# Scale on TensorE in four groups, shift on VectorE, and late constants moved into the first stage of a mixer and mixture-of-experts kernel

## The chip, the cores and the metric

The kernel runs on one core of a Trainium2 chip. The metric is the device time of one execution in microseconds (us). Five engines work in parallel, each through its own queue of instructions in order: PE (TensorE, matmuls; its weight loads are listed apart as PEld), DVE (VectorE), ACT (ScalarE), POOL (GpSimd) and SP (SyncE, which in this kernel only issues DMA loads). They wait for each other through semaphores. SBUF is the on-chip memory, PSUM holds what PE writes.

## The reference, cut to what matters

One layer: 256 tokens, width 1024, a modulated mixer and then 32 experts of which each token takes 4. The part that the change touches is the first line of the layer.

```python
cond = jax.nn.silu(c)
mod = cond @ w_ada[layer] + b_ada[layer]
sh_m, sc_m, g_m, sh_f, sc_f, g_f = [m[:, None, :] for m in jnp.split(mod, 6, axis=-1)]
h = rms_norm(x, norm_mix[layer]) * (1.0 + sc_m) + sh_m
x = x + g_m * hybrid_mixer(h, w_in[layer], ...)      # lru, diff attention, sliding-window attention
h = rms_norm(x, norm_ffn[layer]) * (1.0 + sc_f) + sh_f
x = x + g_f * moe_ffn(h, w_router[layer], b_router[layer], w1[layer], b1[layer], w2[layer], b2[layer])
```

So the mixer's input needs two vectors of 1024, the scale `sc_m` and the shift `sh_m`, each a product of the row `cond` with a 1024 x 1024 matrix, before the first projection can start.

## The kernel before

The mixer takes the first quarter of the time, the experts' weight stream the rest. In the mixer every weight block of 128 x 1024 is split into a high and a low part (`split`, whi by a cast on ACT L117, wlo by a subtraction on DVE L109), and each product is three matmuls (`mm3`, L124 to L126: high x high, low, low).

The first stage is the loop over d = 0..7 in `branches`; d is the chunk of 128 of the 1024 input channels. One pass of it (a "turn" here) is:

- Loads on SP: two halves of the modulation matrix for chunk d (`wada<-wad`, L198, 0.5 MB each) and the projection weights `wqkv[d]` (`wt<-wqkv`, L84, 0.9 MB). The `wt` blocks live in three slots, so a load waits until the turn three before has finished splitting its block. SP waits in its queue for that, and everything queued behind it waits too.
- `ada_rows`: 8 fp32 matmuls (L240; 16 records in the trace) that make scale and shift of the chunk as rows in four column groups, a copy on ACT (`rd`, L243), 2 matmuls with `pick` (L245) that turn the rows into columns, and DVE's `mod` (L247).
- `h_chunk`: A (L253), hd = x * A + shift (L255) on DVE, the high part of h by a cast on ACT (L256), the low part on DVE (L257).
- 24 matmuls (L124 to L126) in the order of the columns of `wqkv`: 12 against its first 1024 columns, 12 against the last 768. They add to seven banks of PSUM that stay open over all eight turns.

Ahead of turn 0 stand the root-mean-square of x (`normed_T`: a Square on ACT for each half of x, sqrt, reciprocal) and 16 transposes of the normed x (L229). After the loop come `csb` (`row_tile`, L526: silu(c) spread over all partitions by 8 matmuls, for the later modulation on DVE), `proj_ch(0)`, the norms of q and k, `late_constants` (rows, gw, wr, b1t, tri and the bias table `relb`), `attn_prepare` (the vector lambda), `bias_tiles` (a product with the bias table, an addition L265, a write to DRAM `scr` from POOL's queue and three loads `tz` of 0.5 MB each through POOL's queue), the projection for the window attention, the diff attention, the lru and the gates. The remaining modulation vectors are made on DVE by a fused product and sum over 1024 columns (L206, output `wada`, one per 128 channels; their loads are `wada<-wada`). `wch` are the 1 MB weight blocks of the later projections.

Nothing in the code fixes the order of instructions of one engine: the Tile framework's scheduler works it out from the program's order, priorities and its own estimate of when operands are ready, when the kernel is built. `tc.high_priority()` lifts what is written inside it. At run time each engine goes through its list strictly in that order.

Of the kernel before, what the change touches and what calls it, by code (L numbers as in the profile page):

```python
# [44 lines left out]
class Kernel:  # L45
# [82 lines left out]
    def constants(self):  # L128
        nc, a, const = self.nc, self.a, self.const
        self.x = self.keep.tile([128, 2, D], F32, name="x")  # L130
        for t in range(2):
            nc.sync.dma_start(out=self.x[:, t], in_=a["x"][t * 128:(t + 1) * 128])
# [42 lines left out]
    def silu_c(self):  # L175

        nc = self.nc
        c = self.col(C_C, 8)
        sc = self.mix.tile([128, 8], F32, name="sc")
        nc.scalar.activation(sc, c, AF.Tanh, scale=0.5)  # L180
        nc.vector.scalar_tensor_tensor(sc, sc, 1.0, c, op0=ALU.add, op1=ALU.mult)
        self.sc = sc
        self.pick = self.early.tile([128, 1], F32, name="pick")
        nc.vector.memset(self.pick, 0.0)
        for j in range(4):
            nc.vector.memset(self.pick[32 * j:32 * j + 1], 1.0)
        self.bm = self.early.tile([128, 8, 2], F32, name="bm")
        b = self.col(C_BADA, 16).rearrange("p (d s) -> p d s", s=2)
        nc.vector.tensor_scalar(self.bm[:, :, 0], b[:, :, 0], 1.0, None, op0=ALU.add)
        nc.vector.tensor_copy(self.bm[:, :, 1], b[:, :, 1])  # L190
        self.mod = self.keep.tile([128, 48], F32, name="mod")

    def ada_load(self, i, first=False):
        ws = []
        for j in range(2):
            ws.append(self.p4("wada") if first else self.p4p.tile([128, D], F32, name="wada", tag="wada", bufs=2))
            src = self.a["wad0"][i] if first else self.a["wada"][i - 8]
            self.nc.sync.dma_start(out=ws[j], in_=src[:, j * D:(j + 1) * D])  # L198
        return ws

    def ada(self, i, ws=None):

        nc = self.nc
        for j, w in enumerate(ws or self.ada_load(i)):
# [4 lines left out]
    def normed_T(self, out):  # L209
# [4 lines left out]
        for t in range(2):  # L214
            nc.scalar.activation(xn[t], self.x[:, t], AF.Square, accum_out=ss[:, t:t + 1])
        self.silu_c()
        rs = mw.tile([128, 2], F32, name="rs")
        self.rstd(rs, ss, D, mw, 2)
        for t in range(2):
            if t:  # L220
                nc.scalar.mul(xn[t], self.x[:, t], rs[:, t:t + 1])
            else:
                nc.vector.tensor_scalar(xn[t], self.x[:, t], rs[:, t:t + 1], None, op0=ALU.mult)
        for d2 in range(4):
            p = self.ps()
            for i in range(2):
                for t in range(2):
# [5 lines left out]
    def ada_rows(self, d, ws):  # L233
# [3 lines left out]
        p = self.ps()  # L237
        for k in range(8):
            j = k % 4
            nc.tensor.matmul(p[32 * j:32 * j + 32, :256], self.sc[:, k:k + 1].to_broadcast([128, 32]),  # L240
                             ws[k // 4][:, j * 256:(j + 1) * 256], start=(k < 4), stop=(k >= 4))
        r = self.mw.tile([128, 256], F32, name="rd")
        nc.scalar.copy(r, p[:, :256])  # L243
        for i in range(2):
            nc.tensor.matmul(p[:, 256 + i:257 + i], r[:, i * 128:(i + 1) * 128], self.pick, start=True, stop=True)  # L245
        m = self.mod[:, 2 * d:2 * d + 2]
        nc.vector.scalar_tensor_tensor(m, p[:, 256:258], 0.5, self.bm[:, d], op0=ALU.mult, op1=ALU.add)  # L247

    def h_chunk(self, x, d):
# [3 lines left out]
        nc.vector.tensor_mul(A, self.mod[:, 2 * d:2 * d + 1], self.col(C_NM + d))  # L253
# [307 lines left out]
    def branches(self, br, gl):  # L561
# [25 lines left out]
        self.csb = self.row_tile("silu", self.sc, self.mix)  # L587
# [13 lines left out]
        self.late_constants()  # L601
        self.attn_prepare()
        self.bias_tiles()
# [547 lines left out]
def layout(inp):  # L1151
# [20 lines left out]
    a["wad0"] = wa[:, 1::-1].reshape(8, 128, 2, 8, 128).transpose(3, 1, 0, 2, 4).reshape(8, 128, 2048)  # L1172
# [51 lines left out]
```

## Time and profile before

| | |
|---|---|
| three runs, median (lowest to highest) | 1238.14 us (1238.09 to 1239.74) |
| the profiled execution's own time | 1238.5 us |
| its span | 1236.7 us |
| busy in the span: PE, DVE, ACT | 1125.8 us, 452.7 us, 259.3 us |
| mean DMA rate over the span | 381 GB/s |
| loop over d, from its first matmul to its last | 17.7 to 74.1 us |
| first matmuls of the experts | about 302 us |

Times within the profile are counted from the start of the span. A busy PE is not a PE at its peak, and PE has two clock levels: 1.00 in the profile's clock column is 2.4 GHz, 0.50 is 1.2 GHz. The profile puts each wait down to the instruction that released it. Whole-kernel shares are of little use here, since the mixer is bound by PE and by the chains between engines, and the experts by DMA; the stages have to be read apart.

### The profile page before, as it was taken

How to read it: one execution, taken by the hardware profiler on the slowest of the kernel's cores; microseconds unless marked ns; L12 is line 12 of the kernel's file. 1: busy time of each engine (PE TensorE's matmuls, PEld its weight loads, DVE VectorE, ACT ScalarE, POOL GpSimd, SP SyncE). 2: the span in 40 equal slices, each digit the busy share in tenths (PEclk: the TensorE clock that was granted, in tenths of full speed). 3: DMA queues.
4: the chain of work that ended last, by engine and by line, in shares of the span. 5: the costliest groups of instructions: out<-in, count | busy, mean ns of one | idle time of the engine just before them, and what ended most of it. 6: DMA issues, size and time to landing. Idle time of an engine off the chain costs nothing.

```text
span 1236.7 us, 13932 instructions
## 1 busy us (share of the span) xinstructions
PE 1125.8 (91%) x5719; PEld 552.4 (45%) x5720; DVE 452.7 (37%) x892; ACT 259.3 (21%) x446; POOL 11.0 (1%) x19
## 2 busy tenths in 40 slices
PE   5998999998988999998989798979898989798987
PEld 4787989995333334332323242324233323332333
DVE  3477888974123231231213132403131222121232
ACT  4475668444101011100000010101010100100000
POOL 0000000000010000000000000000000000000000
PEclk9998999998999999999999999999999999999999
DMA  9688467885999999999999999999999999999996
GB/s 376 210 288 299 147 218 264 343 325 219 414 417 425 424 424 426 427 426 425 423 429 424 429 424 424 429 424 424 423 427 427 424 426 424 427 426 426 423 403 237
DMA packets 54718, 470.70 MB, mean 381 GB/s; under 512 B 6048, under 2 KB 8152, under 8 KB 21112
## 3 DMA queue, kind: packets, MB, share of 16 engines
q1 hardware_dynamic: 53112, 466.93, 91.9%
q0 software_dynamic: 528, 1.72, 0.4%
q10 hardware_dynamic: 1008, 1.09, 0.3%
q8 instruction: 47, 0.77, 0.3%
q14 instruction: 23, 0.19, 0.0%
HBM read 468.65 MB, written 1.07 MB: 380 GB/s over the span
## 4 chain that ended last, share of the span: by engine, by line
PE 55%; DMA 41%; DVE 2%; ACT 1%; issue 1%; SPq 0%; DVEq 0%; ACTq 0%
DMA wt<-w2h 31%; PE po L923 10%; PE mm L923 9%; PE ps L943 7%; DMA wt<-w1h 7%; PE ps L956 3%; PE mm L124 3%; PE mm L125 3%; PE mm L126 3%; PE ps L883 3%; DMA wada<-wada 2%; PE ps L850 1%; PE po L125 1%; PE po L126 1%; PE po L124 1%; PE ps L420 1%
## 5 line engine op out<-in xcount | busy, mean ns | idle before, releaser
L923 PE MATMUL po<-wt,xT 128*64 128x512 f32 x992 | 335.7, 599 | 29.1 <-DMA wt<-w1h 29.1
L923 PE MATMUL mm<-wt,xT 128*64 128x512 f32 x992 | 331.4, 594 | 0.0
L943 PE MATMUL ps<-wt,act 128*64 128x512 f32 x992 | 234.3, 614 | 43.0 <-DMA wt<-w2h 36.1
L949 DVE TENSOR_TENSOR y<-ps,gf 64x512 f32<-64x512 f32 x62 | 42.7, 689 | 352.2 <-PE ps L943 351.5
L923 PEld LDWEIGHTS po<-wt,xT 128*64 128x64 f32 x992 | 87.8, 136 | 169.3 <-issue 112.7
L943 PEld LDWEIGHTS ps<-wt,act 128*64 128x64 f32 x992 | 72.7, 140 | 190.0 <-issue 133.6
L923 PEld LDWEIGHTS mm<-wt,xT 128*64 128x64 f32 x992 | 93.0, 137 | 132.5 <-issue 130.8
L853 DVE TENSOR_TENSOR g<-ps,b1t 128x512 f32<-128x512 f32 x31 | 21.4, 691 | 242.9 <-PE ps L850 242.9
L109 DVE TENSOR_TENSOR wlo<-wt,whi 128x1024 fp32r<-128x1024 f32 x72 | 85.6, 1192 | 35.6 <-ACT whi L117 34.4
L117 ACT CAST whi<-wt 128x1024 fp32r<-128x1024 f32 x72 | 73.5, 1023 | 74.4 <-PE ps L126 27.7
L927 ACT COPY hg<-po 128x512 f32<-128x512 f32 x31 | 18.1, 585 | 302.3 <-PE po L923 256.2
L126 PE MATMUL mm<-h,wlo 128*128 128x256 f32 x256 | 73.7, 288 | 0.0
L125 PE MATMUL mm<-h,whi 128*128 128x256 f32 x256 | 73.5, 287 | 0.0
L124 PE MATMUL mm<-h,whi 128*128 128x256 f32 x256 | 73.4, 287 | 0.0
L856 ACT ACTIVATE ps<-g 128x512 f32<-128x512 f32 x31 | 18.6, 601 | 219.9 <-DVE g L854 219.9
L956 PE MATMUL ps<-y,swT 128*128 128x512 f32 (+1 forms) x128 | 58.2, 606 | 6.4 <-DVE y L949 6.4
L958 DVE TENSOR_TENSOR x<-x,ps 128x512 f32<-128x512 f32 x64 | 43.8, 687 | 18.9 <-PE ps L956 18.9
L124 PEld LDWEIGHTS mm<-h,whi 128*128 128x128 f32 x256 | 49.1, 192 | 1.4 <-issue 1.3
L125 PEld LDWEIGHTS mm<-h,whi 128*128 128x128 f32 x256 | 49.0, 191 | 1.1 <-issue 1.0
L126 PEld LDWEIGHTS mm<-h,wlo 128*128 128x128 f32 x256 | 49.0, 192 | 1.0 <-issue 1.0
L886 ACT ACTIVATE xT<-ps,B,A 128x256 f32<-128x256 f32 x32 | 17.3, 564 | 139.1 <-PE ps L883 138.7
L206 DVE CUSTOM_DVE_ANT_0 wada<-wada,silu,cols 128x1024 f32<-128x1024 f32 x32 | 40.8, 1275 | 7.8 <-DMA wada<-wada 7.8
(335 smaller groups left out, 1103.7 us busy)
## 6 DMA issues: line engine op xcount, KB each, us to landing
wt<-w1h SPq DMA_DIRECT2D x93, 2048.0 KB, 29.5
wt<-w2h SPq DMA_DIRECT2D x47, 2048.0 KB, 29.5
wt<-w1h SPq DMA_DIRECT2D x70, 1024.0 KB, 29.6
wt<-w2h SPq DMA_DIRECT2D x33, 1024.0 KB, 31.3
wt<-wch SPq DMA_DIRECT2D x16, 1024.0 KB, 6.7
wada<-wada SPq DMA_DIRECT2D x32, 512.0 KB, 4.7
wada<-wad SPq DMA_DIRECT2D x16, 512.0 KB, 9.4
wt<-wqkv SPq DMA_DIRECT2D x8, 896.0 KB, 8.7
```

The lines of the kernel that those rows point to most:

```text
L109: eng.tensor_tensor(lo, x, hi.bitcast(F32), op=ALU.subtract)
L117: self.nc.scalar.copy(hi, w)
L124: nc.tensor.matmul(out, lhs[0], rhs[0], start=start, stop=False)
L125: nc.tensor.matmul(out, lhs[0], rhs[1], start=False, stop=False)
L126: nc.tensor.matmul(out, lhs[1], rhs[0], start=False, stop=stop)
L206: nc.vector.tensor_tensor_reduce(out=w, in0=w, in1=self.csb, scale=0.5, scalar=self.col(C_BADA + c), op0=ALU.mult, op1=ALU.add, accum_out= ...
L883: nc.tensor.matmul(p[:, i * 256:(i + 1) * 256], self.xs[j][:, t, d * 128:(d + 1) * 128], sel[:, t], start=(t + j == 0), stop=(t + j == 2))
L923: nc.tensor.matmul(p[64 * hf:64 * hf + 64], xT[:, k, i * CAP:(i + 1) * CAP], w[:, (2 * j + hf) * 512:(2 * j + hf + 1) * 512], start=(k == ...
L943: nc.tensor.matmul(py[rows[hf]], act[:, (k % 4) * 2 + k // 4, :], w[:, (2 * i + hf) * 512:(2 * i + hf + 1) * 512], start=(k == 0), stop=(k ...
L949: nc.vector.tensor_mul(self.y[r, hf], py[r], self.gf[r, hf * 512:(hf + 1) * 512])
L956: nc.tensor.matmul(p, swT[r, i, t * 128:(t + 1) * 128], self.y[r, hf], start=True, stop=True)
L958: nc.vector.tensor_add(self.x[:, t, s], self.x[:, t, s], p)
```

## The change

- `constants`: the loads of x get high priority. `normed_T` is split into `normed` and `transposed_x`. The square of x's second half moves from ACT to DVE (a fused product and sum), the table for sqrt is loaded ahead by a dummy activation, and each half of x is normed by DVE and ACT together, 512 columns each.
- The modulation of chunk d is split by kind. `scales`: 8 matmuls of 128 columns a chunk (256 before) on TensorE, for a group of chunks at once: chunk 0 before turn 0, 1 and 2 before turn 1, 3 and 4 before turn 3, 5 to 7 before turn 5; then one copy, one `pick` matmul a chunk and A for the whole group. `shift`: one fused product and sum on DVE a chunk. Their weights are the new arrays `wsc` and `wsh` (0.5 MB a chunk each).
- `csb`, which the shift needs, is made at the start and not after the loop.
- `late_constants` and `attn_prepare` are called in turn 4 and `bias_tiles` in turn 5; before, all three came after the loop.
- The first `wqkv` block is loaded in two pieces.

The diff, cut to its core (in `layout`, `wad0` is replaced by `wsc` and `wsh`, which hold the same numbers):

```diff
+        with self.tc.high_priority():
+            for t in range(2):
+                nc.sync.dma_start(out=self.x[:, t], in_=a["x"][t * 128:(t + 1) * 128])
...
+    def p4_load(self, name, src):
+        w = self.p4("w" + name)
+        self.nc.sync.dma_start(out=w, in_=src)
+        return w
+
+    def shift(self, d, w):
+
+        c = 2 * d + 1
+        self.nc.vector.tensor_tensor_reduce(out=w, in0=w, in1=self.csb, scale=0.5, scalar=self.col(C_BADA + c),
+                                            op0=ALU.mult, op1=ALU.add, accum_out=self.mod[:, c:c + 1])
...
+        nc.scalar.activation(xn[0], self.x[:, 0], AF.Square, accum_out=ss[:, 0:1])
+        nc.vector.tensor_tensor_reduce(out=xn[1], in0=self.x[:, 1], in1=self.x[:, 1], scale=1.0, scalar=0.0,
+                                       op0=ALU.mult, op1=ALU.add, accum_out=ss[:, 1:2])
+        warm = mw.tile([128, 1], F32, name="warm")
+        nc.scalar.activation(warm, ss[:, 0:1], AF.Sqrt, bias=self.eps, scale=1.0 / D)
...
+            nc.vector.tensor_scalar(xn[t][:, :512], x[:, :512], r, None, op0=ALU.mult)
+            nc.scalar.mul(xn[t][:, 512:], x[:, 512:], r)
...
+    def scales(self, ds, ws):
+
+
+        nc = self.nc
+        p, n = self.ps(), len(ds)
+        for i, w in enumerate(ws):
+            for k in range(8):
+                j = k % 4
+                nc.tensor.matmul(p[32 * j:32 * j + 32, i * 128:(i + 1) * 128],
+                                 self.sc[:, k:k + 1].to_broadcast([128, 32]), w[:, k * 128:(k + 1) * 128],
+                                 start=(k < 4), stop=(k >= 4))
+        r = self.mw.tile([128, 384], F32, name="rd", bufs=1)[:, :n * 128]
+        nc.scalar.copy(r, p[:, :n * 128])
+        for i in range(n):
+            nc.tensor.matmul(p[:, 384 + i:385 + i], r[:, i * 128:(i + 1) * 128], self.pick, start=True, stop=True)
+        nc.vector.scalar_tensor_tensor(self.A1[:, ds[0]:ds[0] + n], p[:, 384:384 + n], 0.5,
+                                       self.bm[:, ds[0]:ds[0] + n], op0=ALU.mult, op1=ALU.add)
+        nc.vector.tensor_mul(self.A1[:, ds[0]:ds[0] + n], self.A1[:, ds[0]:ds[0] + n],
+                             self.col(C_NM + ds[0], n))
...
+        with self.tc.high_priority():
+            first = [self.p4_load("sc", a["wsc"][0])], self.p4_load("sh", a["wsh"][0])
+        self.silu_c()
+        self.csb = self.row_tile("silu", self.sc, self.mix)
+        xn, groups = self.normed(), {0: [0], 1: [1, 2], 3: [3, 4], 5: [5, 6, 7]}
         for d in range(8):
-            w = self.ada_load(d, first=True)
+            g = groups.get(d, [])
+            wg, wsh = first if d == 0 else ([self.p4_load("sc", a["wsc"][e]) for e in g],
+                                            self.p4_load("sh", a["wsh"][d]))
+            wt = self.take()[:, :1792]
+            for c in (slice(0, 1024), slice(1024, 1792)) if d == 0 else (slice(0, 1792),):
+                nc.sync.dma_start(out=wt[:, c], in_=a["wqkv"][d][:, c])
+            if g:
+                self.scales(g, wg)
+            self.shift(d, wsh)
             if d == 0:
-                self.normed_T(gl[:2])
-            wt = self.load(a["wqkv"][d])
-            self.ada_rows(d, w)
+                self.transposed_x(xn, gl[:2])
             self.h_chunk(gl[d // 4][:, d % 4], d)
+            if d == 4:
+                self.late_constants()
+                self.attn_prepare()
+            if d == 5:
+                self.bias_tiles()
...
-        self.csb = self.row_tile("silu", self.sc, self.mix)
...
-        self.late_constants()
-        self.attn_prepare()
-        self.bias_tiles()
```

The change moves instructions. First place: PE between turn 0 and turn 1. In the kernel before, PE makes the modulation of chunk 1, and already that of chunk 2, between the last matmuls of turn 0 (into `ps`, 256 columns) and the first of turn 1 (into `mm`):

```order
L125 MATMUL ps<-wlo,h_75 128x256
L126 MATMUL ps<-whi,h_76 128x256
L240 MATMUL ps<-wada,sc 32x256 x8
L245 MATMUL ps<-pick,rd 128x1 x2
L240 MATMUL ps<-wada,sc 32x256 x8
L124 MATMUL mm<-whi,h_75 128x512
L125 MATMUL mm<-wlo,h_75 128x512
```

In the changed kernel the scales of chunks 1 and 2 stand there together, and nothing follows their `pick` until turn 1:

```order
L125 MATMUL ps<-wlo,h_75 128x256
L126 MATMUL ps<-whi,h_76 128x256
L256 MATMUL ps<-wsc,sc 32x128 x16
L262 MATMUL ps<-pick,rd 128x1 x2
L124 MATMUL mm<-whi,h_75 128x512
L125 MATMUL mm<-wlo,h_75 128x512
```

The second set of L240, which made the modulation of a chunk one turn ahead, is gone; each group is made right before the turn that needs it.

Second place: SP's queue from turn 5's loads on. Before, modulation weights and projection weights of a chunk alternate to the last chunk, and only then the `wch` blocks come, with most late constants behind them:

```order
L198 DMA wada<-wad 128x1024 x2
L84 DMA wt<-wqkv 128x1792
L198 DMA wada<-wad 128x1024 x2
L84 DMA wt<-wqkv 128x1792
L84 DMA wt<-wch 128x2048 x2
L149 DMA rows<-rows 128x40
L152 DMA gw<-gw 128x1024
```

In the changed kernel the late constants stand ahead of the scales of chunks 5 to 7, and the last two shift loads (chunks 6 and 7) behind two `wch` loads:

```order
L161 DMA tri<-tri 128x128
L422 DMA lamv<-rows 128x256
L202 DMA wsc<-wsc 128x1024 x3
L202 DMA wsh<-wsh 128x1024
L597 DMA wt<-wqkv 128x1792 x3
L84 DMA wt<-wch 128x2048
L350 DMA lam<-cols 128x4
L197 DMA wada<-wada 128x1024
L84 DMA wt<-wch 128x2048
L202 DMA wsh<-wsh 128x1024 x2
L197 DMA wada<-wada 128x1024 x4
```

What moved: the weights that turns 6 and 7 need for their h stood ahead of all `wch` loads, and half of them now stand behind two.

Third place: DVE ahead of turn 6. Before, between the last split of block 6 (`wlo_553`, from `wt_515`) and hd of chunk 6 (`hd_532`) stand only the small `mod` and A; the first split of block 7 (`wlo_594`) follows:

```order
L109 TENSOR_TENSOR wlo_553<-wt_515,whi_552 128x768
L247 SCALAR_TENSOR_TENSOR mod_142<-ps_517,bm_139 128x2
L253 TENSOR_TENSOR A1_113<-mod_142,cols_107 128x1
L255 TENSOR_SCALAR hd_532<-gl1_87,A1_113,mod_142 128x256
L109 TENSOR_TENSOR wlo_594<-wt_572,whi_593 128x1024
```

In the changed kernel the first split of block 7 (`wlo_629`), a modulation product (`wada_1275`), the small chain `sp` of the lru and the shift of chunk 6 (`wsh_578`, read from its load) stand ahead of hd of chunk 6 (`hd_583`):

```order
L109 TENSOR_TENSOR wlo_629<-wt_621,whi_628 128x1024
L356 TENSOR_SCALAR sp_1190<-sp_1190 128x4
L216 ISA wada_1275,mod_136<-wada_1275,silu_137,cols_107 128x1024
L216 ISA mod_136 128x1
L357 RECIPROCAL sp_1190<-sp_1190 128x4
L358 TENSOR_TENSOR sp_1190<-sp_1190 128x4
L359 TENSOR_TENSOR sp_1190<-sp_1190 128x4
L360 TENSOR_SCALAR sp_1190<-sp_1190 128x4
L362 SCALAR_TENSOR_TENSOR sp_1190<-sp_1190 128x4 x7
...
L208 ISA wsh_578,mod_136<-wsh_578,silu_137,cols_107 128x1024
L208 ISA mod_136 128x1
L273 TENSOR_SCALAR hd_583<-gl1_87,A1_113,mod_136 128x256
```

What moved: these came after the loop before (`wada`, `sp`) or did not exist on DVE (`wsh`).

## Rows read from the trace of the kernel before

**Rows 1.** Busy time by stage: stretch, its length, engines' busy us, PEclk, DMA share, GB/s.
```profile
150.00:290.00 140.00, 140.00 (x1030) 128.35 (x1030) 113.96 (x178) 83.33 (x139) 0.10 (x1) 1.00 0.78 293
290.00:308.00 18.00, 12.70 (x72) 8.27 (x72) 9.09 (x35) 9.21 (x18) 2.51 (x2) 0.81 0.21 90
350.00:1236.00 886.00, 800.12 (x3574) 292.58 (x3570) 227.43 (x423) 77.48 (x135) 3.57 (x4) 0.99 1.00 418
```

**Rows 2.** The same view, stretches after the loop.
```profile
75.00:95.00 20.00, 18.99 (x139) 17.26 (x137) 18.71 (x47) 17.02 (x30) 0.00 (x0) 1.00 0.80 266
113.00:118.00 5.00, 1.70 (x15) 1.50 (x13) 2.83 (x11) 2.14 (x5) 0.00 (x0) 0.89 0.83 315
118.00:127.00 9.00, 8.97 (x35) 7.25 (x36) 5.63 (x18) 3.48 (x9) 0.00 (x0) 0.50 0.64 227
```

**Rows 3.** Waits of PE from 0 to 120 us: total, times, longest.
```profile
PE ps L430 <- ACT e L424: 3.3, 1, 3.3
```

**Rows 4.** Timeline of DVE at 115 us: start, length, what, idle before it.
```profile
115.14 1.28 DVE L206 CUSTOM_DVE_ANT_0 wada<-wada,silu,cols 128x1024 f32<-128x1024 f32 x1 [3.93 <-DMA wada<-wada]
```

**Rows 5.** Chain of waits, 105 to 130 us, and loads by line (last: us to landing).
```profile
103.37 11.74 DMA wada<-wada
...
wt<-wch SPq DMA_DIRECT2D x1, 1024.0 KB, 4.9
...
wt<-wch SPq DMA_DIRECT2D x1, 1024.0 KB, 9.1
```

**Rows 6.** Chain of waits, start to turn 0: start, length, what.
```profile
10.12 3.86 PE ps L229 x16
...
15.31 0.38 ACT rd L243
15.73 0.62 PE ps L245 x4
16.84 0.42 DVE hd L255
17.28 0.41 ACT h L256
17.74 0.68 PE mm L124
```

**Rows 7.** Busy time by stage, 17 to 28 us.
```profile
17.00:28.00 11.00, 9.44 (x61) 6.70 (x61) 4.12 (x8) 3.90 (x6) 0.00 (x0) 0.84 1.03 423
```

**Rows 8.** Chain of waits: before turn 1, first matmuls of turns 1, 3 and 4.
```profile
24.46 1.04 PE ps L240 x16
...
27.96 0.50 PE mm L124
...
41.66 0.50 PE mm L124
...
48.51 0.50 PE mm L124
```

**Rows 9.** Timeline of PE: start of turn 7 and end of the loop.
```profile
69.05 0.50 PE L124 MATMUL mm<-whi,h 128*128 128x512 f32 x1
...
74.07 1.05 PE L526 MATMUL ps<-kst,sc 128*128 128x128 f32 x8
```

**Rows 10.** Timeline of SP and of DVE around turns 5 and 6, and after the loop.
```profile
53.52 7.17 SPq L84 DMA_DIRECT2D wt<-wch  x2
...
59.38 0.96 DVE L109 TENSOR_TENSOR wlo<-wt,whi 128x768 fp32r<-128x768 f32 x1 [2.86 <-ACT whi L117]
...
77.81 1.28 DVE L206 CUSTOM_DVE_ANT_0 wada<-wada,silu,cols 128x1024 f32<-128x1024 f32 x1
```

**Rows 11.** DVE's groups, 62 to 100 us: line, count, busy us, mean ns.
```profile
L344 DVE SCALAR_TENSOR_TENSOR sp<-sp 128x4 f32<-128x4 f32 x7 | 1.1, 157 | 0.2
```

**Rows 12.** Timeline of PE: five small matmuls of the router.
```profile
295.93 0.18 PE L750 MATMUL ps<-maskb,trib 128*128 128x32 bf16 x1 [2.78 <-DVE maskb L748]
...
296.03 0.19 PE L754 MATMUL ps<-maskb,oneb 128*128 128x32 bf16 x1
```

More of the change, by code (lines that the diff above doesn't have):

```diff
@@ L130, in constants @@
         self.x = self.keep.tile([128, 2, D], F32, name="x")
-        for t in range(2):
-            nc.sync.dma_start(out=self.x[:, t], in_=a["x"][t * 128:(t + 1) * 128])
+        with self.tc.high_priority():
+            for t in range(2):
+                nc.sync.dma_start(out=self.x[:, t], in_=a["x"][t * 128:(t + 1) * 128])
         self.cols = const.tile([128, N_COLS], F32, name="cols")
@@ L186, in silu_c, with ada_load, ada @@
             nc.vector.memset(self.pick[32 * j:32 * j + 1], 1.0)
-        self.bm = self.early.tile([128, 8, 2], F32, name="bm")
+        self.bm = self.early.tile([128, 8], F32, name="bm")
         b = self.col(C_BADA, 16).rearrange("p (d s) -> p d s", s=2)
-        nc.vector.tensor_scalar(self.bm[:, :, 0], b[:, :, 0], 1.0, None, op0=ALU.add)
-        nc.vector.tensor_copy(self.bm[:, :, 1], b[:, :, 1])
+        nc.vector.tensor_scalar(self.bm, b[:, :, 0], 1.0, None, op0=ALU.add)
         self.mod = self.keep.tile([128, 48], F32, name="mod")
-    def ada_load(self, i, first=False):
+    def ada_load(self, i):
         ws = []
         for j in range(2):
-            ws.append(self.p4("wada") if first else self.p4p.tile([128, D], F32, name="wada", tag="wada", bufs=2))
-            src = self.a["wad0"][i] if first else self.a["wada"][i - 8]
-            self.nc.sync.dma_start(out=ws[j], in_=src[:, j * D:(j + 1) * D])
-        return ws
-    def ada(self, i, ws=None):
+            ws.append(self.p4p.tile([128, D], F32, name="wada", tag="wada", bufs=2))
+            self.nc.sync.dma_start(out=ws[j], in_=self.a["wada"][i - 8][:, j * D:(j + 1) * D])
+        return ws
+    def p4_load(self, name, src):
[6 more added lines that the diff above has]
+                                            op0=ALU.mult, op1=ALU.add, accum_out=self.mod[:, c:c + 1])
+    def ada(self, i):
         nc = self.nc
-        for j, w in enumerate(ws or self.ada_load(i)):
+        for j, w in enumerate(self.ada_load(i)):
             c = 2 * i + j
@@ L207, in ada, with normed @@
                                            op0=ALU.mult, op1=ALU.add, accum_out=self.mod[:, c:c + 1])
-    def normed_T(self, out):
+    def normed(self):
         nc, mw = self.nc, self.mw
@@ L213, in normed_T @@
         ss = mw.tile([128, 2], F32, name="ss")
-        for t in range(2):
-            nc.scalar.activation(xn[t], self.x[:, t], AF.Square, accum_out=ss[:, t:t + 1])
-        self.silu_c()
+        nc.scalar.activation(xn[0], self.x[:, 0], AF.Square, accum_out=ss[:, 0:1])
[3 more added lines that the diff above has]
+        nc.scalar.activation(warm, ss[:, 0:1], AF.Sqrt, bias=self.eps, scale=1.0 / D)
         rs = mw.tile([128, 2], F32, name="rs")
@@ L219, in normed_T, with transposed_x @@
         for t in range(2):
[L220 to L223, printed above, removed]
+            x, r = self.x[:, t], rs[:, t:t + 1]
+            nc.vector.tensor_scalar(xn[t][:, :512], x[:, :512], r, None, op0=ALU.mult)
+            nc.scalar.mul(xn[t][:, 512:], x[:, 512:], r)
+        return xn
+    def transposed_x(self, xn, out):
+        nc = self.nc
         for d2 in range(4):
             p = self.ps()
-            for i in range(2):
-                for t in range(2):
+            for t in range(2):
+                for i in range(2):
                     d = 2 * d2 + i
@@ L231, in normed_T @@
             nc.scalar.copy(out[d2 // 2][:, d2 % 2 * 2:d2 % 2 * 2 + 2], p.rearrange("p (i m) -> p i m", i=2))
-    def ada_rows(self, d, ws):
+    def scales(self, ds, ws):
         nc = self.nc
[L237 to L247, printed above, removed]
+        p, n = self.ps(), len(ds)
[13 more added lines that the diff above has]
+                             self.col(C_NM + ds[0], n))
     def h_chunk(self, x, d):
@@ L252, in h_chunk @@
         A = self.A1[:, d:d + 1]
-        nc.vector.tensor_mul(A, self.mod[:, 2 * d:2 * d + 1], self.col(C_NM + d))
         h = self.mw.tile([128, T], F32, name="hd")
@@ L1171, in layout @@
         .reshape(16, 128, 2048)
-    a["wad0"] = wa[:, 1::-1].reshape(8, 128, 2, 8, 128).transpose(3, 1, 0, 2, 4).reshape(8, 128, 2048)
+    a["wsc"] = wa[:, 1].reshape(8, 128, 8, 128).transpose(2, 1, 0, 3).reshape(8, 128, 1024)
+    a["wsh"] = wa[:, 0].transpose(1, 2, 0)
     oh, neg = _bucket_rows()
```

## The prediction

> **What bounds the kernel now.** I read the busy time by stage first. From 150 to 290 us PE is busy all of 140 us, so the mixer there is as long as its matmuls [rows 1]. From 290 to 308 us the DMA share is 0.21, from 350 us to the end it is 1.00 [rows 1]: the experts are a stream of weights that stops for the mixer's end and then runs without a break. Whatever the mixer gains or loses therefore reaches the end of the kernel one to one, and only PE's path through the first 150 us can change. Three things stand in that path. First, before turn 0 PE waits for the chain of x and modulation: transposes at 10.12, copy of the modulation rows at 15.31, `pick` at 15.73, hd at 16.84, h at 17.28, first matmul at 17.74 [rows 6]. Second, the boundaries between turns: a turn's own 24 matmuls take 74.07 - 69.05 = 5.02 us [rows 9], turns 3 and 4 start 48.51 - 41.66 = 6.85 us apart [rows 8], so a boundary costs 1.83 us, in which PE makes modulation. The boundary before turn 1 is 27.96 - 24.46 = 3.5 us [rows 8]. Third, the stretch 113 to 127 us. The list of PE's waits has one of 3.3 us there, for an exp on ACT [rows 3]; DVE shows why: it had stood 3.93 us for the load of a modulation block, with the scores queued behind [rows 4], a load issued at 103.37 that took 11.74 us [rows 5] beside the bias tiles `tz`. After it PE runs at a granted clock of 0.50 (1.2 GHz) from 118 to 127 us, 8.97 us busy [rows 2], so half of 9 us, 4.5 us, is lost as well. DVE is nearly full from 75 to 95 us, 18.71 of 20 [rows 2].
>
> **The start.** The copy, `pick` and `mod` of chunk 0 (15.31 to 16.84 [rows 6]) now run before the transposes and leave the path. Against this DVE does two fused products of 1.28 us each, a length I take from the same operation later [rows 10], ahead of the reciprocal: the square of the second half of x, and the shift of chunk 0, which stands before it in DVE's order. One Square and one table load leave ACT. I put the transposes at 11.5 instead of 10.12, add their 3.86 and about 1 us for the last copy, hd 0.42 and h 0.41 [rows 6], and get turn 0 at 16.4: -1.3 us, with -2.5 and 0 as ends.
>
> **The boundaries up to turn 5.** A chunk's modulation took 1.04 us on PE for 256 columns [rows 8]; the scale alone has 128, so 0.52 a chunk. But it is made right before the turn that needs it, and then the chain copy (0.42 to the next start), `pick` (0.62 for two columns), A, hd, h (17.74 - 16.35 = 1.39) [rows 6] stands bare. Before turn 1: 2 x 0.52 + 0.42 + 0.62 + 1.39 = 3.5. Before turn 3 the same with a small operation of DVE more: 3.6. Before turn 5, three chunks: 1.56 + 0.55 + 0.93 + 1.39 = 4.4. Turns 2 and 4 follow at once. Sum 11.5 against 3.5 + 4 x 1.83 = 10.8: +0.7. Halving the columns buys nothing here, since its saving is paid back as latency. With the start, turn 5 ends at 59.8, where it ended at 48.51 + 6.85 + 5.02 = 60.4.
>
> A price that no row shows is the clock in these three gaps. Before turn 0 PE stood 0.4 and 1.39 us around its `pick`, and the granted clock of 17 to 28 us was then 0.84 [rows 6, 7]: (1 - 0.84) x 2 x 11 = 3.5 us at half clock, 1.8 us lost. The old boundary before turn 1, in which PE made the modulation of two chunks [rows 8], lies in the same stretch and cannot have cost more than that sum. The new gaps hold the idle pieces of the first and the matmuls of half the second. Between 0 and 3 x 1.8 = 5.4 I take two of three, +3.6, as they are nearer to the first.
>
> **Turn 6.** Here I see the largest loss. The loads of the shifts of chunks 6 and 7 now stand on SP behind a `wch` load that waits for a weight slot. That slot comes free when the last split of block 6 is done; before, the split ran at 59.38 for 0.96, and SP's two `wch` loads, begun at 53.52, were through 7.17 us later, at 60.7 [rows 10]. Now 0.6 earlier: the `wch` load leaves at 59.7 and the shift loads behind it. Alone, 1 MB landed 4.9 us after its issue [rows 5], and half a MB more at 418 GB/s [rows 1] makes 1.2: 65.8. But the three `tz` loads, moved into turn 5, leave POOL's queue at about the same time. Beside `tz`, 1 MB took 9.1 and the modulation load 11.74 [rows 5]. I take 9.1 for the shift load, as it is the next half MB behind 1 MB: 68.8 landed, ends 65.8 and 71.4. DVE alone cannot be ready much sooner: it first has the split of block 7, whose buffer comes free at turn 5's end (cast and split, about 2.2 by the 0.96 of the smaller split), one modulation product 1.28 [rows 10] and 15 small operations of the lru at 0.157 [rows 11], so 59.8 + 2.2 + 1.3 + 2.4 = 65.7. After the load: shift 1.28, hd 0.42, h 0.41, and a few tenths between: turn 6 at 71.2 (68.1 to 73.6), PE idle 11.4 us. The third matmul waits 0.6 more, since the low part of h stands behind the shift of chunk 7. After such a pause the clock will be low: 1.8 us lost as at turn 0 [rows 7], up to the 4.5 of 118 to 127 us [rows 2]; I take 1.8, since turns 6 and 7 are dense as turn 0 was. From there turns 6 and 7 run together and no `csb` follows: 71.2 + 10.0 + 0.6 + 1.8 = 83.6 for the first projection after the loop, against 74.9: +8.7.
>
> **After the loop.** The `tz` loads are over long before the scores, so the wait of 3.3 us [rows 3] and the 4.5 us at half clock behind it [rows 2] should go: -7.8. Next late there is DVE: the order brings modulation products forward, and the stage 75 to 95 us had 1.3 us of DVE and 1.0 us of PE to spare [rows 2]. That can give the 1.0 back or cost some 3 us (two or three products of 1.28 in front of a norm); I count 0.
>
> **Sum.** +8.7 (start, boundaries and turn 6 are in it) + 3.6 (clock in the gaps) - 7.8 = +4.5. On the profiled execution, 1238.5 with 1.8 outside its span of 1236.7, that is 1243.0; the median lies 0.4 lower: **1242.6**.
>
> **A rule against the halved columns.** Five small matmuls of the router start within 0.10 us, 25 ns apart [rows 12], and 16 records of a chunk in 0.52 us would be 32 ns apart, so I see no floor in the way. The Trainium skill, "TensorE: Matmul & The Clock Gate", section "Wait — 56ns, not 53.3ns?", names two floors for small matmuls, about 25 ns start to start, and about 62 ns where the sequencer decodes each. By the second, 16 records cost 0.99 us and the halved columns would save next to nothing, giving about 1246; rows 12 agree with the first.
>
> **Rivals.** (a) About even. One of the two largest unknowns falls well: the `tz` loads leave SP's queue alone and the shift load lands at 65.8, so that DVE sets turn 6 at 68.1 (-3.1), or the clock holds in the gaps (-3.6). Sum +0.9 to +1.4, 1239.0 to 1239.5. For it: `tz` leaves late in turn 5 and may find the `wch` load half through. Against: 9.1 for 1 MB in the only case where both met.
> (b) Faster: a short pause at full clock. If the shift load lands before DVE has done its 65.7 us of work, the load has no price at all, and if PE then also keeps 2.4 GHz over the three gaps, the sum is +4.5 - 3.1 - 3.6 = -2.2, and with the 1.0 us of PE's idle time after the loop -3.2: 1235. It decides at a landing of 65.7. For it: the chunk groups are dense on both sides; against: turn 0 lost its clock after idle pieces of the same lengths. Should the pause before turn 6 not exist at all, turn 7 ends at 69.8 instead of 83.6, and the time is near 1229.
> (c) The halved columns save nothing: seven chunks on the path at 0.52 more, +3.6, 1246.2.
> (d) It doesn't do what it is laid out for: a modulation load in 105 to 118 us is late without `tz` too, because SP's queue waits for slots. Then the 7.8 stay: 1250.
>
> **How the numbers follow.** Forecast 0.38, (a) 0.29, (b) 0.24, (c) 0.04, (d) 0.05. A measurement of this kernel can tell about 0.2%, 2.5 us, from no change. Slower: forecast, (c) and (d), 0.47; within: 0.29; faster: 0.24. The forecast's own range is 1240.7 to 1246. The range for all goes down to (b) with a little more, 1233.5, and up to turn 6 at 73.6 with all three gaps at half clock, 1242.6 + 2.4 + 1.8, and part of DVE's 3 us: 1248. Outside I leave 0.10 below and 0.08 above.
>
> **What would show it.** In the changed kernel: turn 0 near 16.4; gaps of 3.5, 3.6 and 4.4 us before turns 1, 3 and 5, with the granted clock below 1.00 behind them; SP waiting for a split with a `wch` load around 52 to 60 us; DVE waiting for `wsh` near 66 to 69 and turn 6 near 71; no wait of PE for exp near 115 to 125, and clock 1.00 there. I am wrong if turn 6 follows turn 5 within 5 us, or if PE's stretch 75 to 150 us is lengthened by DVE by more than 3 us.

## The result and the profile after

The changed kernel takes 1245.91 us (median of 5, 1244.48 to 1247.97) against 1238.14 for the kernel before: ratio 1.0065, 95% interval 1.0054 to 1.0076. It is slower by 0.65%, 7.8 us. The forecast was slower, 1242.6, with a range of 1233.5 to 1248. Of the executions of the experiments below, one of e10_products_doubled took 2286.74 us; its ratio leaves it out.

The profiled execution took 1244.48 us (span 1242.7), 6.0 more than that of before. Four moments divide the difference: the first matmul of turn 0 (17.15, before 17.74), the end of turn 5 (63.8, before 60.4), the first projection after the loop (88.48, before 74.88) and the first expert matmul (307.91, before 302.06). The loop loses 13.6 us, the rest of the mixer wins 7.75 back, and the experts add nothing: 1244.48 - 307.91 = 936.6, before 1238.5 - 302.06 = 936.4.

PE's starts of turns 1, 3, 5 and 6 and of the first projection, from its timeline, with the idle time ahead in brackets:

```profile
27.34 0.79 PE L124 MATMUL mm<-whi,h 128*128 128x512 f32 x1 [1.40 <-ACT h L274]
...
42.77 0.50 PE L124 MATMUL mm<-whi,h 128*128 128x512 f32 x1 [1.71 <-ACT h L274]
...
57.21 0.50 PE L124 MATMUL mm<-whi,h 128*128 128x512 f32 x1 [0.27 <-ACT h L274]
...
75.49 0.80 PE L124 MATMUL mm<-whi,h 128*128 128x512 f32 x1 [11.57 <-ACT h L274]
...
88.48 0.28 PE L124 MATMUL mm<-h,whi 128*128 128x256 f32 x1
```

The 11.57 us ahead of turn 6 is the pause. What it waited for is seen step by step on three engines. SP's timeline: the `wch` load, held until 63.76 (the last split of block 6, on DVE, ended at 63.74), and the two shift loads behind it.

```profile
63.76 0.33 SPq L84 DMA_DIRECT2D wt<-wch  x1
64.19 1.09 SPq L202 DMA_DIRECT2D wsh<-wsh  x2
```

DVE's timeline: its work ahead of the shift of chunk 6 was over at 70.3, and it stood 2.95 us for the load; the shift starts at 73.25 and hd follows.

```profile
70.14 0.16 DVE L368 TENSOR_SCALAR spn<-sp 128x4 f32<-128x4 f32 x1
73.25 1.29 DVE L208 CUSTOM_DVE_ANT_0 wsh<-wsh,silu,cols 128x1024 f32<-128x1024 f32 x1 [2.95 <-DMA wsh<-wsh]
...
74.58 0.41 DVE L273 TENSOR_SCALAR hd<-gl,A,mod 128x256 f32<-128x256 f32 x1
```

And the chain of waits between 0 and 90 us goes through the load itself; the `tz` loads were issued from POOL at 61.17, as its timeline shows:

```profile
64.19 9.04 DMA wsh<-wsh
```
```profile
61.17 2.32 POOL L289 DMA_DIRECT2D tz<-scr  x3 [1.50 <-DMA scr<-relb]
```

The busy time by stage (stretch, length, busy us of PE, PEld, DVE, ACT, POOL, granted clock, DMA share, GB/s) shows the clock behind the gaps: half behind the first and the third, full behind the second, and half for 6.5 us behind the pause.

```profile
28.00:30.00 2.00, 2.00 (x6) 1.58 (x5) 2.00 (x4) 0.00 (x0) 0.00 (x0) 0.50 0.86 322
...
42.00:45.00 3.00, 2.23 (x10) 1.75 (x11) 2.16 (x8) 2.21 (x4) 0.00 (x0) 1.00 0.88 357
...
59.00:60.00 1.00, 1.00 (x4) 0.80 (x3) 0.00 (x0) 0.00 (x0) 0.67 (x1) 0.50 0.00 0
...
75.50:82.00 6.50, 6.50 (x15) 4.73 (x16) 4.11 (x9) 1.09 (x2) 0.00 (x0) 0.50 0.48 152
```

After the loop there is hardly a wait left. From 75 to 250 us PE's list of waits holds, beside the pause that ends at 75.49, only the two lines of the first fence; the wait for exp [rows 3] is not among them. The stretch from 113 us that had 1.70 of 5 us busy and then 9 us at half clock [rows 2] starts 13.6 us later here, behind the longer loop, and now reads as in the second fence (same columns):

```profile
PE ps L342 <- DVE rs L173: 0.2, 1, 0.2
PE mm L124 <- ACT gl L647: 0.2, 1, 0.2
```
```profile
125.00:135.00 10.00, 9.99 (x75) 8.57 (x74) 8.88 (x27) 6.54 (x16) 0.00 (x0) 1.00 0.84 276
135.00:150.00 15.00, 15.00 (x111) 12.87 (x111) 13.59 (x48) 9.52 (x26) 0.00 (x0) 1.00 0.72 260
```

### The profile page after: what moved, and what is told of

It reads as the page before. It is cut to its first block, busy times and chain, and to the rows that moved or that the text cites. A ratio compares the mean times of both kernels' runs of the same rounds, so it can differ in the third digit from the quotient of the medians.

```text
span 1242.7 us, 13898 instructions
## 1 busy us (share of the span) xinstructions
PE 1123.7 (90%) x5703; PEld 552.7 (44%) x5704; DVE 462.4 (37%) x902; ACT 251.9 (20%) x438; POOL 10.7 (1%) x19
## 4 chain that ended last, share of the span: by engine, by line
PE 56%; DMA 39%; DVE 2%; ACT 1%; issue 1%; SPq 0%; ACTq 0%; DVEq 0%
DMA wt<-w2h 23%; DMA wt<-w1h 14%; PE po L953 10%; PE mm L953 9%; PE ps L973 8%; PE ps L986 4%; PE mm L124 4%; PE mm L126 3%; PE mm L125 3%; PE ps L913 3%; PE po L125 1%; PE po L124 1%; PE po L126 1%; PE ps L880 1%; PE ps L438 1%; DMA wsh<-wsh 1%
## 5 line engine op out<-in xcount | busy, mean ns | idle before, releaser
L886 ACT ACTIVATE ps<-g 128x512 f32<-128x512 f32 x31 | 18.6, 602 | 219.9 <-DVE g L884 219.9
```

## The experiments

Two questions were open. Is the pause before turn 6 really the place of two loads in SP's queue, and which part of the change put them there? And what sets the stretch from the first projection after the loop to the first expert matmul (called "the rest" below), where the change wins: the bias tiles' loads alone, or DVE, which had done five modulation products (5 x 1.28 us) by 88.48 and none by 74.88 in the kernel before? The ratios are against runs of the kernel before on the same chip.

| kernel | median us | ratio, 95% interval | loop's end | first expert matmul | the rest |
|---|---|---|---|---|---|
| before | 1238.14 | | 74.88 | 302.06 | 227.2 |
| changed | 1245.91 | 1.0065, 1.0054 to 1.0076 | 88.48 | 307.91 | 219.4 |
| e1_shift_early | 1238.07 | 1.0007, 0.9992 to 1.0022 | 74.46 | 298.55 | 224.1 |
| e2_late_back | 1240.17 | 1.0028, 1.0015 to 1.0041 | 73.06 | 303.02 | 230.0 |
| e3_late_alone | 1255.49 | 1.0138, 1.0110 to 1.0166 | 96.50 | 318.40 | 221.9 |
| e5_both | 1238.80 | 1.0007, 0.9994 to 1.0021 | 74.44 | 301.11 | 226.7 |
| e6_bias_turn7 | 1235.59 | 0.9982, 0.9972 to 0.9992 | 77.59 | 302.18 | 224.6 |
| e7_best | 1237.30 | 0.9995, 0.9985 to 1.0004 | 72.62 | 299.43 | 226.8 |
| e8_late7_alone | 1241.37 | 1.0029, 1.0019 to 1.0038 | 77.20 | 306.71 | 229.5 |
| e9_products_early | 1238.73 | 1.0009, 0.9997 to 1.0021 | 77.33 | 300.73 | 223.4 |
| e10_products_doubled | 1232.49 | 0.9952, 0.9936 to 0.9968 | 74.66 | 294.56 | 219.9 |
| e11_changed_doubled | 1244.45 | 1.0049, 1.0032 to 1.0066 | 88.29 | 309.38 | 221.1 |
| e12_filled_gaps | 1234.22 | 0.9969, 0.9957 to 0.9982 | 73.56 | 297.05 | 223.5 |
| e13_filled_doubled | 1230.79 | 0.9938, 0.9921 to 0.9954 | 75.17 | 295.19 | 220.0 |

The last three columns are from the one profiled execution of each kernel, whose time can lie 3 us off the median (e1: 1234.9, e6: 1238.7). What comes behind the last column took 936 to 938 us, so differences between the columns do not add up exactly to those between the medians.

**Shift loads early.** The two loads are called in turn 5, ahead of the bias tiles.

```diff
+            elif d == 5:
+                wg, last = [self.p4_load("sc", a["wsc"][e]) for e in g], \
+                    {e: self.p4_load("sh", a["wsh"][e]) for e in (5, 6, 7)}
+            if d > 4:
+                wsh = last[d]
```

> The changed kernel, with the shift loads of chunks 6 and 7 called in turn 5, right behind that of chunk 5 and ahead of the bias tiles; nothing else differs, but the order puts them ahead of the last three projection blocks on SP. My theory (the pause of 11.5 us before turn 6 is the two loads standing behind a waiting wch load): DVE waits for no wsh, turn 6 follows turn 5 within 2 us, the first projection after the loop starts at 72 to 76 instead of 88.5, and the time falls by 10 to 15 us against the changed kernel, to 1230 to 1235. Rival (DVE is too full before turn 6: split, modulation product and the lru's small operations lasted to 70.1 in the changed kernel): turn 6 still starts after 70, and the time falls by 4 us at most, to about 1241.

SP now issues them at 33.3, behind the scales' loads; DVE waits for no `wsh`, no pause, and the loop ends at 74.46 as my theory had it. SP's timeline:

```profile
33.34 4.28 SPq L202 DMA_DIRECT2D wsh<-wsh  x3
37.72 9.99 SPq L604 DMA_DIRECT2D wt<-wqkv  x3
60.16 5.20 SPq L84 DMA_DIRECT2D wt<-wch  x2
```

The rival is out: DVE's work does not hold turn 6 once the loads are there. But the whole wins 7.8 us against the changed kernel and not 10 to 15, since the rest is 4.7 us longer.

**Late constants back after the loop.** The three calls return to their old place, ahead of the projection for the window attention; scale, shift and start stay as in the change.

```diff
-            if d == 4:
-                self.late_constants()
-                self.attn_prepare()
-            if d == 5:
-                self.bias_tiles()
...
+        self.late_constants()
+        self.attn_prepare()
+        self.bias_tiles()
```

> The changed kernel with late constants, lambda and bias tiles called after the loop again, as before the change. My theory: the shift loads keep their place ahead of the wch loads, no pause before turn 6, first projection after the loop at 73 to 75; but the bias tiles load beside the modulation loads again, so that the wait of PE for exp and the half clock behind it come back, 7.8 us at most: 1236 to 1240, about the kernel before. Rival (the new form of scale and shift with its bare chains is what costs): the time stays above 1241.

No pause, loop end 73.06, and a wait of 3.4 us in the scores is back. PE's waits from 0 to 300 us:

```profile
PE mm L124 <- ACT h L274: 5.2, 4, 2.5
PE ps L438 <- DVE st L440: 3.4, 1, 3.4
```

So the new form of scale, shift and start, alone, ends the loop 1.8 us earlier and has a rest 2.8 us longer: slower than before by 0.28%, just above the 1236 to 1240 that I expected and below the rival's 1241.

**Late constants alone.** The kernel before with only the three calls moved.

```diff
             self.h_chunk(gl[d // 4][:, d % 4], d)
+            if d == 4:
+                self.late_constants()
+                self.attn_prepare()
+            if d == 5:
+                self.bias_tiles()
```

> The kernel before with one part of the change alone: late constants and lambda called in turn 4, bias tiles in turn 5. My theory: the bias tiles take three buffers of the pool that the modulation weights use, so that the loads of chunks 6 and 7 slip behind two wch loads here too; PE waits about 11 us for the modulation of chunk 6, the wait for exp after the loop is gone: 1242 to 1246. Rival (the late constants are harmless where they now stand, and only the new shift on DVE makes the pause): 1229 to 1232.

This decides which part of the change it is: the three moved calls, and not the new shift. Without any shift on DVE the loads of the modulation of chunks 6 and 7 slip behind the second `wch` load (SP's timeline, first fence), and PE stands for them (its timeline, second fence). It is 17 us slower than before, more than the whole change and more than I expected. Scale and shift come in one array there, so four loads of 0.5 MB are late instead of two, and behind the 10.64 us of the second fence PE still has to make the modulation: turn 6 starts only at 78.30, with a granted clock of 0.55 from 72 to 84 us.

```profile
61.81 0.33 SPq L84 DMA_DIRECT2D wt<-wch  x1
62.23 2.05 SPq L198 DMA_DIRECT2D wada<-wad  x4
```
```profile
72.61 1.08 PE L240 MATMUL ps<-wada,sc 128*32 128x256 f32 x8 [10.64 <-DMA wada<-wad]
```

**Early shift loads, and scales in the middle of the turn before.** On top of the first edit:

```diff
             self.tokens_k(pq, self.h, d, hi[:, 512:], lo[:, 512:])
+            if d + 1 in groups:
+                n = groups[d + 1]
+                self.scales(n, [self.p4_load("sc", a["wsc"][e]) for e in n])
```

> The changed kernel with the shift loads of chunks 6 and 7 early as in the first of these runs, and each group of scales called between the second and third quarter of the matmuls of the turn before, so that copy, pick, A, hd and h run beside matmuls. My theory (the chains cost three gaps of 3.5 to 4.5 us and two stretches at half clock): no gap above 1 us before turns 1, 3 and 5, clock 1.00 from 22 us on, first projection after the loop at 63 to 67, the time 1220 to 1226. Rival (DVE, with one shift product a turn, is the bound of the loop once the gaps are gone, or what is gained is given back after the loop on DVE): 1228 or more.

Missed by far, already in the loop, which ended at 74.44 and not at 63 to 67. The chain of waits shows why: with scale made early, the shift product of the chunk is now what stands ahead of hd (turn 1 here), and three of them follow each other before turn 5 (50.57, 52.31 and 54.62). PE's longest wait there, 3.75 us ahead of turn 5, is for a split on ACT, which stands behind h of chunk 6.

```profile
23.45 1.20 DVE wsh L208
24.78 0.42 DVE hd L273
25.22 0.41 ACT h L274
25.68 0.50 PE mm L124
...
50.57 1.20 DVE wsh L208
...
54.62 1.19 DVE wsh L208
```

**Bias tiles in turn 7.** One number of the change: `if d == 5` becomes `if d == 7` at `bias_tiles()`.

> The changed kernel with one call moved: bias tiles in turn 7 and not in turn 5, so that the shift loads of chunks 6 and 7 take their buffers before the bias tiles do and stand on SP ahead of the wch loads again. My theory: no pause before turn 6, DVE never waits for wsh, the wait for exp after the loop stays away since the bias tiles still land by 85; the three gaps with their half clock stay. First projection after the loop at 72 to 75, time 1232 to 1236. Rival (what the early shift loads gave back in the first of these runs, DVE too full from 75 to 125 us, is the true bound): 1237 to 1240 again.

The slip is gone with that alone, and the kernel is faster than before by 0.18%; no PE wait between the loop and the router is longer than 1.9 us. The loop's end in the profiled execution, 77.59, is later than I said, because the clock was low behind all three gaps there (0.85 from 28 to 62 us, 0.65 from 61.2 to 66) and the third gap was 5.8 us long, not 4.4.

**Scales in mid-turn, everything late in turn 7.** The edit of the mid-turn scales, with all three late calls at `d == 7`.

> The changed kernel with late constants, lambda and bias tiles all called in turn 7, and each group of scales called in the middle of the turn before. My theory: no gap over 1.5 us between turns, clock 1.00 from 22 us on, first projection after the loop at 63 to 67, the bias tiles landed by 80, no wait for exp over 1 us; 1222 to 1230. Rival (DVE or the loads after the loop set the pace, so that an earlier end of the loop is given back): 1234 to 1240.

Loop end 72.62, not 63 to 67. The idle pieces ahead of turns 1, 3 and 5 are 2.03, 1.10 and 1.44 us (1.40, 1.71 and 0.27 in the changed kernel, which has copy and `pick` ahead of them too), and the clock of 28 to 62 us is 0.97. So the gaps shrink, but ahead of turns 1 and 5 h still waits for a shift (on DVE at 23.63 and 51.82). The rest takes 226.8 and gives it back.

**Late constants in turn 7, alone.** The kernel before with the three calls at `d == 7`.

> The kernel before with late constants, lambda and bias tiles called in turn 7, nothing else of the change. My theory: the modulation loads of chunks 6 and 7 keep their place ahead of the wch loads (the slip needs the bias tiles to take their buffers first), the loop ends at 74 as before, and the wait for exp with its half clock is gone: 1230 to 1234. Rival (that wait comes from the modulation loads themselves, or something else is late next): 1236 to 1240.

The loads keep their place, no long pause shows and the last turn ends at 74.4 as expected (the 77.20 of the table holds both halves of `csb` and a wait of 0.9 us too), but the kernel is slower than before by 0.29%: my theory missed here. The wait for exp is gone from PE's list (its largest there is one of 2.0 for a split), yet others take its place, 6.4 us in all and 4.3 of half clock, and the rest is longer than before. Moving the bias tiles is thus not worth 7.8 us by itself.

**What sets the rest.** By now its length went from 219 to 230 us over kernels that do the same work there. I took DVE for the cause and made two tests: less of its work in that stage, and more.

```diff
+            for j in {4: [8], 6: [9]}.get(d, []):
+                self.ada(j)
...
-            self.ada(8 + i)
```

> The kernel with bias tiles in turn 7, and with the first four modulation products of the stage after the loop (and their loads) called in turns 4 and 6 of the loop, where DVE has idle time. My theory (after the loop DVE is the engine that is late next, so that an earlier end of the loop is given back there unless DVE has done products ahead, as it had during the pause of the changed kernel): 5.1 us of DVE's work leave that stage, the time from the first projection after the loop to the first expert matmul falls from 224.6 to 220 to 222, time 1231 to 1234. Rival (PE's own work or the loads are late next): no change against the kernel with bias tiles in turn 7, 1235 to 1237.

```diff
+            if i < 10:
+                u = self.mw.tile([128, 1], F32, name="spare", tag="spare")
+                nc.vector.tensor_tensor_reduce(out=w, in0=w, in1=self.csb, scale=0.5, scalar=0.0,
+                                               op0=ALU.mult, op1=ALU.add, accum_out=u)
```

> The kernel with bias tiles in turn 7, and the first four modulation products after the loop done twice on DVE (the second result is not used): 5.1 us more of DVE's work, no load and no matmul more. My theory (DVE is late next in that stage): the time rises by 3 to 5 us to 1238 to 1241. Rival (DVE's idle time takes it): within 1.5 us of the kernel with bias tiles in turn 7, up to 1237.

Both went against me. Four products fewer: slower than the kernel with bias tiles in turn 7 (1238.73 against 1235.59), though the rest of the profiled execution is 1.2 us shorter. Four products more: faster, 1232.49, with the rest at 219.9 and DVE busy 10.00 of 10 us from 85 to 95. The same doubling in the changed kernel itself:

> The changed kernel itself with the same four products done twice. My theory (the pause before turn 6 let DVE run ahead by five products, which is why PE waited only 0.2 us from the loop's end to 290 us): the slack takes part of the 5.1 us, and the pause itself grows by at most one product: the time rises by 0 to 3 us, to 1246 to 1249, less than where there is no pause. Rival (the 7.8 us won back after the loop came from the bias tiles alone, and DVE has the same slack in both): the same rise as in the kernel without the pause.

1244.45 against 1245.91: no rise at all, so this run tells the two theories apart as little. "DVE has too much to do" falls. What does hold in all fourteen profiles is a sum. From the loop's end to 12.5 us before the first expert matmul (where the router begins) I added PE's idle time and what half clock cost, (1 - granted clock) x length, both from the busy time by stage: before 4.65 + 4.3, changed 0.6 + 0, e2 7.1 + 4.3, e6 4.4 + 2.1, e8 6.4 + 4.3, e10 1.7 + 0, e12 4.4 + 0. The rest minus that sum is 217.9 to 219.5 in every kernel. (The clock column has two decimals, over some 210 us a step of 2.1 us; added up over slices of 2 us, the half clock of these seven comes to 5.1, 0, 3.4, 1.7, 5.1, 0 and 0, and the remainder of all to 217.4 to 219.5.) This is bookkeeping: PE has nearly the same matmuls in each kernel, its own work is some 95% of the stage or more, and what differs is single waits and the clock behind them. Where a wait comes from the sum does not say. A row of e6 and the answering one of e10 show the difference: 1.4 us idle with a granted clock of 0.83, against none and 1.00.

```profile
95.00:105.00 10.00, 8.57 (x35) 7.03 (x36) 8.12 (x17) 4.87 (x10) 0.00 (x0) 0.83 0.64 227
```
```profile
95.00:105.00 10.00, 10.00 (x61) 8.68 (x60) 9.87 (x17) 6.90 (x11) 0.00 (x0) 1.00 0.72 216
```

Most edits, also those in the loop, give the scheduler another order of the 310 to 345 instructions of DVE in this stage, and the waits there changed with it. Products done ahead do not decide it either: by the loop's end DVE had begun five in the changed kernel, and one each in e6 and e10, whose rests are 224.6 and 219.9. Why one order has waits and another not is open.

**Matmuls in the gaps.** Six fp32 matmuls of 112 columns behind each `pick` of a group, results unused, on top of the bias tiles in turn 7 (first) and of the doubled products (second).

```diff
+        if n > 1:
+            for i in range(6):
+                nc.tensor.matmul(p[:, 400:512], self.ident, self.kst[:, :112], start=True, stop=True)
```

> The kernel with bias tiles in turn 7, and six fp32 matmuls of 112 columns (their result is not used) behind the pick of each group of two or three chunks, so that PE is busy while A, hd and h are made before turns 1, 3 and 5; no wait is removed. My theory (what a gap costs is its idle time and, behind it, a stretch at half clock of 3 to 3.5 us, which goes if PE has matmuls in the gap): granted clock 1.00 from 24 to 75 us, gaps as long as before (within 0.3 us), the loop ends 1.5 to 4 us earlier than 77.6. Rival (the clock falls whatever PE does in 1.4 of 3.5 us, or the filling lengthens the gaps): loop end within 1 us of 77.6. The order after the loop is another one, so the whole time says little: 1229 to 1238.

> The kernel with the four products done twice (1232.5, the fastest so far), with the same filling of the gaps. My theory: clock 1.00 in the loop from 24 us on, loop end 1.5 to 4 us before 74.7. After the loop, if the shape of the order and not DVE's load decides, the stretch from the loop's end to the first expert matmul can be anything from 219 to 230 us although DVE has the same work: 1228 to 1240. Rival (DVE's work sets it): as long as without the filling, 219 to 221.

Half right. PE's timeline of the first: the filling runs from 24.70 and 38.59, and turns 1 and 3 follow it without a wait. Its busy time by stage: full clock behind the first two gaps, half behind the third all the same.

```profile
24.70 1.59 PE L269 MATMUL ps<-kst 128*128 128x112 f32 x12 [0.32 <-DVE A L263]
38.59 1.59 PE L269 MATMUL ps<-kst 128*128 128x112 f32 x12 [0.36 <-DVE A L263]
```
```profile
28.00:34.00 6.00, 6.00 (x30) 5.01 (x29) 3.19 (x5) 1.88 (x2) 0.00 (x0) 1.00 0.98 284
...
56.00:62.00 6.00, 6.00 (x16) 4.03 (x15) 4.24 (x7) 0.12 (x1) 2.26 (x3) 0.60 0.04 7
```

The loop ended at 73.56 against 77.59, but 75.17 against 74.66 in the second, where the third gap was followed by half clock for the whole of 56 to 62 us. So in both filled kernels no half clock came behind the first and second gap, and in both it came around the third. Set beside the unfilled kernels, this is firm for the first gap alone. In the seven with these gaps (changed, e1, e2, e6, e9, e10 and e11) the clock of the three us from the start of turn 1 is 0.50 to 0.71, in the two filled ones 1.00. From the start of turn 3 it is 1.00 in four of the seven anyhow, and from the start of turn 5 it is 0.50 to 0.69 in all nine.

In time, the filling won 1.6 us behind the first gap, lengthened that gap by 0.3, and lengthened the third by 1.1 to 1.2 us, where it fell to half clock itself (2.27 us in e12, against 1.59 in the first two gaps). The rest of the 4.0 us between e6 and e12 is 2.7 behind the second gap, where e10 had full clock without any filling, and 1.4 from turn 0, ahead of the first filling. After the loop the two pairs show what an unchanged order does: the filled kernels' lists of DVE and ACT instructions there are those of e6 and e10, but for one or two records, and so is PE's idle time, 4.4 us against 4.4 and 2.0 against 1.7. 1230.79 (0.9938) is the fastest of all kernels run, with useless products and matmuls in it; of those with only useful work it is the one with the bias tiles in turn 7, 1235.59.

## Why the prediction was right, step by step

- **What bounds the kernel.** Right: the experts took 936.6 us after the mixer, 936.4 before, so each us of the mixer came out at the end.
- **The start.** -0.6, forecast -1.3, within its ends. PE's transposes began at 13.03 and not 11.5: the spread of silu(c) over the rows, which the shift needs, took 3.75 us on PE from 6.67 (one half of it 1.05 later in the loop of before [rows 9]), so that DVE began the shift only at 11.07 and the reciprocal came behind it at 12.28. The cause I had named (the shift ahead of the reciprocal) was there, later than I put it.
- **The boundaries.** Right. Gaps of 3.6, 3.9 and 4.4 us, forecast 3.5, 3.6 and 4.4. A group of two chunks took 1.05 us on PE, three 1.49, as the halved columns should: 16 records in 0.52 us are 33 ns apart. The Trainium skill, "TensorE: Matmul & The Clock Gate", section "Wait — 56ns, not 53.3ns?", names a floor of about 62 ns a matmul where the sequencer decodes each; it did not show.
- **The clock in the gaps.** Right in number: two of three, the first and the third. The second gap is a draw, though: behind it the clock fell in three of the seven unfilled kernels with these gaps (e6, e9 and e11), behind the other two gaps in all seven.
- **Turn 6.** Right. Forecast: `wch` load at 59.7, shift load 9.1 us to landing, DVE ready at 65.7, pause of 11.4. Measured: 63.76 (about 3.2 of the 4.1 later by the clock of the gaps, 0.7 by the later start), 9.04, 70.3, 11.57. That the bias tiles make the load slow was taken from one row of before [rows 5]. It was met again in so far as the 1 MB `wch` load issued at 52.70, ahead of the bias tiles, landed in 4.8 us and the one at 63.76, beside them, in 8.2; no run has the slip without the bias tiles, so their share of the 9.04 was not measured by itself. The step that was under-sized is the clock behind the pause: 6.5 us at half, 3.25 lost, where I took 1.8 and had 4.5 as the end.
- **After the loop.** -7.75, forecast -7.8, and the sum of idle time and half clock, 8.95 before and 0.6 after, is nearly that gain. But the reason was too simple: I put it down to the bias tiles loading early. In e1, e6 and e8, where they load early as well and no pause stands before, the rest is 224.1, 224.6 and 229.5, so 3.1 and 2.6 us are won and 2.3 lost. The wait for exp goes in each of them; but PE's other idle time, 1.35 us before, which I counted as unchanged with 3 us more as the bad end, is 5.8, 4.4 and 6.4. That the -7.8 was met so closely is therefore in part luck. Why the changed kernel has almost no such idle time is open; that the pause helped it, by letting DVE run ahead, was argued and not shown.
- **The sum.** +4.5 forecast on the profiled execution, +6.0 measured. The 1.5 us are 0.7 from the start, 0.3 from the pause, 0.6 from turns 6 and 7 (1.45 by the clock behind the pause, less 0.5 since the third matmul waited 0.1 us and not 0.6, and 0.35 since both turns were a little shorter than 5.0), 0.2 after the loop, and -0.35 from the start of turn 0 to the end of turn 5, where the gaps were 0.4 longer and half clock cost less than 3.6. So small misses cancelled in part. The median of the runs lies 1.4 above the profiled execution.
- **The part I had not seen.** I read from SP's order that the loads stand behind `wch`, but not why. e6, where only the call of `bias_tiles` differs, shows that it is the place of that call; e3 shows it without the shift, and e1 that loads called ahead of it keep their place. By the code, its three tiles come from the same pool of nine buffers as the weights of the modulation. That chunks 6 and 7 get their buffers, and so their place in the queue, after them because they are called after them is my reading and not shown; with a pool of its own it was not tried.

## What to carry to other kernels

When loads that belong to a later stage are called early, look in the built order at what is called after them: here one early call, whose tiles share a pool with the loop's weights, put the loads of two later turns behind a waiting one in the same queue. Moving the call by two turns of the loop was worth 10 us here. And when a stage's length changes with every edit elsewhere, add up the idle time and half clock of the bound engine before naming a cause: here a test with more work on the suspected engine came out faster.

## What the runs showed of the hardware

- The first of two loads of 0.5 MB issued at 64.19, behind one of 1 MB issued at 63.76 in its own queue and beside three of 0.5 MB issued from 61.17 on another, took 9.04 us to land; DVE's shift took 1.28 us in the loop as after it.
- Granted clock of 0.50 (1.2 GHz) came behind gaps of 3.6 to 4.4 us in which PE ran 1.7 to 3.2 us of small matmuls, in two of three gaps of the changed kernel, and in all three of e6, the third of which was 5.8 us long; with fp32 matmuls in the first gap as well the clock was 1.00 behind it (e12 and e13), where it was 0.50 to 0.71 in seven kernels without; behind a pause of 11.57 us it lasted for 6.5 us of dense matmuls.
- The 16 fp32 matmuls that spread silu(c), the first work of PE in the execution, were slower than the same form later, though the granted clock reads 1.00 from 6 to 11 us. The times of line 544 in the changed kernel (shortest, median and longest duration in ns, first and last start in us); no run tells why:

```profile
L544 PE MATMUL ps<-kst,sc x16: 411/421/550, 6.7 to 10.0; 128*128 128x128 f32 x16
L544 PE MATMUL ps<-kst,gm x16: 275/275/356, 240.7 to 242.5; 128*128 128x128 f32 x16
```
